# Two layers of a streaming encoder on one core: an earlier norm sum, seven PSUM banks for MLA's input projection, and a last down projection with tokens on partitions

## The chip, the cores and the metric

The kernel runs on one core of one Trainium2 chip. The metric is the device time of one execution in microseconds (us), the median over runs. TensorE is called PE in the rows of the profile (PEld is its weight load), VectorE DVE, ScalarE ACT, GpSimd POOL, and SyncE SP; SP issues all the DMAs spoken of here.

## The reference, cut to what matters

Two layers of an encoder trunk are computed for 256 prompt frames and for 8 sequences of 16 new frames with caches, together N = 384 tokens of D = 1024 features. All is float32.

```python
for layer in range(2):
    y = y + 0.5 * swiglu_ffn(y, ffn1_norm[layer], ffn1_w_gu[layer], ffn1_w_down[layer])
    h = rmsnorm(y, mix_norm[layer])
    if layer == 0: y = y + even_merge(a_attend(...), b_attend(...), ...)   # two kinds of attention
    else:                                                                # multi-head latent attention (MLA)
        cq, ckv, kr = split(h @ c_w_in, [384, 640])    # 384 | 256 | 32 columns
        q = rmsnorm(cq, g_q) @ w_q_up;  ckv = rmsnorm(ckv, g_kv);  kr = rope(kr)
        y = y + c_attend(q, expand(ckv), kr) @ c_w_out
    y = y + 0.5 * swiglu_ffn(y, ffn2_norm[layer], ffn2_w_gu[layer], ffn2_w_down[layer])
return rmsnorm(y, final_norm), and the new keys, values and latents

def swiglu_ffn(x, g, w_gu, w_down):                    # w_gu 1024 x 5632, w_down 2816 x 1024
    gate, up = split(rmsnorm(x, g) @ w_gu, 2)
    return (silu(gate) * up) @ w_down
```

## The kernel before, in words

Activations lie transposed: the residual is eight SBUF tiles x0 to x7, each 128 features by 384 tokens. Each float32 product is made as three matmuls in a faster format: both operands are split into a high and a low part (h and l in the names: xh, xl for normed-to-be activations, wh, wl for weights, gh, gl for the gated values), and `mm3` adds h·h, h·l and l·h into one PSUM bank. ACT makes the high part (CAST, or ACTIVATE with the norm's gain as scale), DVE the low part by subtraction. `load_w` does this for a weight block of 128 x 1024: a DMA into one of three raw buffers, then cast and subtraction into one of three split buffers.

A norm is applied late. `Sub.push` scales x by the gain alone and adds its square to `ssq` (class `Stats`). `Stats.rstd` then sums over the partitions by a float32 matmul of ones with ssq into the PSUM bank T and makes 1/sqrt on DVE and ACT (`ms`, a root on ACT, a reciprocal and four small steps on DVE). The projections go on meanwhile and are multiplied by rstd when DVE reads them from PSUM. So until rstd is there, every finished projection holds its bank.

PSUM has eight banks: three named acc, two S, two L, one T. `acc_tile` hands out the three acc banks in turn, and `ring_tile` hands out all seven.

The four FFNs are one function, `ffn`. It runs over the 22 blocks f of 128 hidden features: a gate and an up projection of 24 matmuls each (8 feature blocks by 3), then g = gate·rstd on DVE, Silu on ACT, u = up·rstd and u·silu on DVE, and the split into gh, gl. The first two projections run interleaved (`pair`). In the very first FFN four run interleaved (`together`), as the weights arrive, and the call of `rstd` stands behind the first further pair. The squares of this first norm are made on POOL (`push(d, True)`), all others on ACT with the sum on POOL. The down projection then runs over the 8 output blocks d of 128 features: 22 x 3 matmuls of 384 columns with the weights as the stationary operand, and DVE adds half of the result to x[d].

In `mla_mixer` five projections of c_in (three for cq, two for ckv) and a narrow one for kr precede a chain on DVE: rstd, cq, ckv, their norms' sums (`rc_m`), a reciprocal root by integer start and three Newton steps (`rc_t`, `rc_o`), and `spread`, which makes diagonal tiles `dg` that a float32 matmul with ones turns into rows (bank acc). The query-up projections (cqh, cql with q_up weights) are next on TensorE, and DVE can read them only when `te` and `to`, made from the spread, are there.

After the last FFN the final norm sums the squares over features with small matmuls, spreads 1/rms over the partitions, and DVE multiplies eight tiles y, each followed by its store (1.5 KB runs, transposed on the host afterwards).

The tile framework orders the instructions of each engine by its own simulation, within the bounds of data and buffers; engines then run their queues in order.

Of the kernel before, what the change touches and what calls it, by code (L numbers as in the profile page):

```python
# [11 lines left out]
F32 = mybir.dt.float32  # L12
F32R = mybir.dt.float32r
I32 = mybir.dt.int32
AF = mybir.ActivationFunctionType
# [20 lines left out]
LAM_INIT = 0.8 - 0.6 * math.exp(0.0)  # L36
CH = 1024

G_FFN1, G_MIX, G_FFN2, G_FIN, G_CQ, G_CKV, G_SUB = 0, 16, 32, 48, 56, 59, 61
G_N = 62  # L40
C_ID, C_COMB, C_BM, C_M0, C_TE, C_TO = 0, 128, 192, 200, 202, 586
C_N = 970

# [23 lines left out]
def trunk(ctx, tc, I, O):  # L67
# [13 lines left out]
    def acc_tile():  # L81
        return ps_a.tile([P, 512], F32, name="acc")
# [72 lines left out]
    def rsqrt(out, ms, shape):  # L155
        r, n = shape
        t = tmp.tile([P, N], F32, name="rs_t", bufs=1)[:r, :n]
        nc.scalar.sqrt(t, ms)
        nc.vector.reciprocal(out, t)  # L159
        nc.vector.tensor_tensor(out=t, in0=ms, in1=out, op=ALU.mult)  # L160
        nc.vector.tensor_tensor(out=t, in0=t, in1=out, op=ALU.mult)
        nc.vector.tensor_scalar(t, t, -0.5, 1.5, op0=ALU.mult, op1=ALU.add)
        nc.vector.tensor_tensor(out=out, in0=out, in1=t, op=ALU.mult)
# [64 lines left out]
    class Sub:  # L228
# [4 lines left out]
            self.g = g  # L233

        def push(self, d, onpool=False):
            if self.g is None:
                if d < KT - 1:
                    self.stats.add(x[d])
                return
            h = nrm.tile([P, N], F32R, name=f"xh{d}", tag=f"xh{d}")  # L240
            l = nrm.tile([P, N], F32R, name=f"xl{d}", tag=f"xl{d}")
            g = gcol(self.g + d)
            nc.scalar.activation(h, x[d], AF.Copy, scale=g)
            nc.vector.scalar_tensor_tensor(l, x[d], g, h.bitcast(F32), op0=ALU.mult, op1=ALU.subtract)  # L244
            self.h[d], self.l[d] = h, l
            self.stats.add(x[d], onpool)
# [18 lines left out]
    def pair(sub, w0, w1, new=ring_tile):  # L265
        return together(sub, lambda k: (blk(w0, k), blk(w1, k)), new)
# [2 lines left out]
        nc.vector.scalar_tensor_tensor(x[d], ps[:, :N], coef, x[d], op0=ALU.mult, op1=ALU.add)  # L269


    def ffn(sub, gu, down, g_next, pre=()):
        with tc.tile_pool(name="ffn", bufs=1) as fp, tc.tile_pool(name="ffnt", bufs=2) as ft:
            gt = []
            held = []
            rstd = None
            if pre:
                g0, u0, g1, u1 = together(sub, lambda k: [blk(pre[k // 2], 4 * (k % 2) + c) for c in range(4)])
                held = [(0, g0, u0), (1, g1, u1)]
            for f in range(len(held), FT):  # L280
                wg = load_w(gu[2 * f])
                if f == 0:
                    held.append((0, *pair(sub, wg, load_w(gu[1]))))
                    continue
                pg = proj(sub, wg, new=ring_tile)
                pu = proj(sub, load_w(gu[2 * f + 1]), new=ring_tile)
                held.append((f, pg, pu))
                if rstd is None:
                    rstd = sub.stats.rstd(D)
                for f_, pg, pu in held:  # L290
                    g = ft.tile([P, N], F32, name="g")
                    s = ft.tile([P, N], F32, name="s")
                    u = ft.tile([P, N], F32, name="u")
                    nc.vector.tensor_tensor(out=g, in0=pg[:, :N], in1=rstd, op=ALU.mult)  # L294
                    nc.scalar.activation(s, g, AF.Silu)
                    nc.vector.tensor_tensor(out=u, in0=pu[:, :N], in1=rstd, op=ALU.mult)
                    nc.vector.tensor_tensor(out=u, in0=u, in1=s, op=ALU.mult)
                    h = fp.tile([P, N], F32R, name=f"gh{f_}")
                    l = fp.tile([P, N], F32R, name=f"gl{f_}")
                    split(u, h, l)  # L300
                    gt.append((h, l))
                held = []
            nxt = Sub(g_next)
            for d in range(KT):
                ps = ring_tile()
                for c0 in range(0, FT, 8):
                    n = min(8, FT - c0)
                    w = load_w(down[d][:, c0 * P:(c0 + n) * P], n * P)
                    for j in range(n):
                        k = c0 + j  # L310
                        mm3(ps[:, :N], blk(w, j), gt[k], k == 0, k == FT - 1)
                add_resid(ps, d, 0.5)
                nxt.push(d)
            return nxt
# [298 lines left out]
    def mla_mixer(sub, g_next):  # L613
        with ExitStack() as es:
# [15 lines left out]
            cst = Stats()  # L630
            cqs = []
            slot = lambda shape, dt, name, tag: mp.tile(shape, dt, name=name, tag=tag)
            two = pair(sub, load_w(I["c_in"][0]), load_w(I["c_in"][1]), acc_tile)
            for i in range(3):
                ps = two.pop(0) if two else proj(sub, load_w(I["c_in"][i]))
                if rstd is None:
                    rstd = sub.stats.rstd(D)
                t = slot([P, N], F32, f"cq{i}", ("oh7", "ol7")[i % 2])
                nc.vector.tensor_tensor(out=t, in0=ps[:, :N], in1=rstd, op=ALU.mult)  # L639
                cst.add(t)  # L640
                g = gcol(G_CQ + i)
                h = slot([P, N], F32R, f"cqh{i}", f"oh{i}")
                l = slot([P, N], F32R, f"cql{i}", f"ol{i}")
                nc.scalar.activation(h, t, AF.Copy, scale=g)
                nc.vector.scalar_tensor_tensor(l, t, g, h.bitcast(F32), op0=ALU.mult, op1=ALU.subtract)
                cqs.append((h, l))
# [2 lines left out]
            cks = [(slot([P, NP], F32R, f"ckvh{i}", f"oh{3 + i}"), slot([P, NP], F32R, f"ckvl{i}", f"ol{3 + i}"))  # L649
                   for i in range(2)]  # L650
            for i in range(2):
                ps = proj(sub, load_w(I["c_in"][3 + i]))
                nc.vector.tensor_tensor(out=ckv[:, i], in0=ps[:, :N], in1=rstd, op=ALU.mult)
                kst.add(ckv[:, i])
            w = load_w(I["c_kr"], 512)
# [191 lines left out]

    sub = Sub(G_FFN1)
    for d in range(KT):
        sub.push(d, True)  # L850
    nc.sync.dma_start(out=con, in_=I["con"])
    sub = ffn(sub, I["gu0"], I["dn0"], G_MIX, first_w)
    sub = even_mixer(sub, G_FFN2)
    sub = ffn(sub, I["gu1"], I["dn1"], G_FFN1 + 8)
    sub = ffn(sub, I["gu2"], I["dn2"], G_MIX + 8)
    sub = mla_mixer(sub, G_FFN2 + 8)
    sub = ffn(sub, I["gu3"], I["dn3"], None)
    sq = tmp.tile([P, N], F32, name="sq")
    nc.scalar.sqrt(sq[:, 0:1], ones[:, 0:1])
    nc.scalar.activation(sq, x[KT - 1], AF.Square)  # L860
    pc = acc_tile()
    sub.stats.sums(pc, 0, stop=False)
    sub.stats.sums(pc, 0, sq, start=False)
    ms = tmp.tile([P, 16], F32, name="rc_m")[:, :3]
    nc.vector.tensor_scalar(ms, pc[:, :3], 1.0 / D, EPS, op0=ALU.mult, op1=ALU.add)
    rc = nrm.tile([P, 16], F32, name="rc_o", bufs=2)[:, :3]
    rsqrt(rc, ms, (P, 3))
    rb = spread(rc, 0)
    for d in range(KT):
        y = nrm.tile([P, N], F32, name=f"y{d}", tag=f"xh{d}")  # L870
        nc.vector.scalar_tensor_tensor(y, x[d], gcol(G_FIN + d), rb[:, :N], op0=ALU.mult, op1=ALU.mult)  # L871
        nc.sync.dma_start(out=O["y"][d * P:(d + 1) * P], in_=y)

# [24 lines left out]
def _host(i):  # L900
# [2 lines left out]
    o = {}  # L903
    xx = np.concatenate([A["x_prompt"][0], A["x_sample"].reshape(NS, D)], 0)
    o["xT"] = f(xx.T.reshape(KT, P, N).transpose(1, 0, 2))
    cols = [A["ffn1_norm"], A["mix_norm"], A["ffn2_norm"], A["final_norm"], A["c_q_norm"], A["c_kv_norm"], A["b_subln"]]
    o["gains"] = f(np.concatenate([a.reshape(-1, P) for a in cols], 0).T)
    o["con"] = _consts()
    for l in range(2):
        for n, nm in enumerate(("ffn1", "ffn2")):  # L910
            g = A[nm + "_w_gu"][l].reshape(KT, P, 2, FT, P).transpose(3, 2, 1, 0, 4)
            o[f"gu{2 * l + n}"] = f(g).reshape(2 * FT, P, KT * P)
            d = A[nm + "_w_down"][l].reshape(FT, P, KT, P).transpose(2, 1, 0, 3)
            o[f"dn{2 * l + n}"] = f(d).reshape(KT, P, FF)
    e = A["e_w_in"][0].reshape(KT, P, 6, 4, P)
    o["e_in"] = f(e[:, :, [0, 1, 3, 4]].transpose(2, 3, 1, 0, 4)).reshape(16, P, KT * P)
    o["e_v"] = f(e[:, :, [2, 5]].transpose(2, 1, 0, 3, 4)).reshape(2, P, KT * 512)
# [37 lines left out]
    return o  # L955


_OUT = {"y": (D, N), "ak": (512, N), "av": (N, 512), "bk": (512, N), "bv": (N, 512), "ckv": (256, N), "ckr": (32, N)}


# [21 lines left out]
```

## Time and profile before

| | |
|---|---|
| median of 3 runs | 1512.06 us (1512.0 to 1515.81) |
| the profiled execution | 1511.95 us, span 1510.2 us |
| busy: PE / DVE / ACT / POOL | 1481.2 / 793.7 / 591.1 / 135.9 us |
| mean granted clock of TensorE | 0.989 |

The span is from the first to the last instruction; the 1.75 us between it and the execution's time lie around the program. Busy time of TensorE is modelled and overlaps from one matmul to the next, so the distance between two starts tells more than a duration. The granted clock is the share of 2.4 GHz that TensorE was given; 0.5 is 1.2 GHz.

### The profile page before, as it was taken

Reading aid. Unit: us, or ns where it says so; the run is one execution under the profiler, and the core shown is the slowest. Engines: PE = TensorE matmul, PEld = TensorE weight load, DVE = VectorE, ACT = ScalarE, POOL = GpSimd, SP = SyncE. Lnnn points to the kernel's source line nnn. Section 1 sums busy time; section 2 is a strip of 40 time slices with the busy share of each in tenths; the row PEclk is TensorE's granted clock in tenths of the full one; section 3 lists DMA queues with packets and bytes.
Section 4 is the critical chain, followed back from the end, with each engine's and each line's share of the span. In section 5 each row is a group of like instructions: output and inputs, shape, how many; then the busy total and the mean of one; then the engine's idle time right before and its main releaser. Section 6 shows DMA issues by size and latency. Waiting matters only on the chain.

```text
span 1510.2 us, 21698 instructions
## 1 busy us (share of the span) xinstructions
PE 1481.2 (98%) x8680; PEld 1443.6 (96%) x8680; DVE 793.7 (53%) x1369; ACT 591.1 (39%) x996; POOL 135.9 (9%) x146
## 2 busy tenths in 40 slices
PE   9899999999999999999999999999899999999997
PEld 9899999998888999999999999999798999999997
DVE  6655543345356755553346555434757466555433
ACT  4433333325345433333334333333367444333231
POOL 5000000114230100000100000011210020000000
PEclk9999999999899999999999999999999999999998
DMA  7333343545443343344433334445231133433341
GB/s 239 110 125 126 126 126 115 171 149 175 145 133 105 120 132 126 126 124 124 129 126 126 126 126 127 124 120 180 86 125 38 62 119 127 130 129 124 116 130 66
DMA packets 71877, 190.09 MB, mean 126 GB/s; under 512 B 6720, under 2 KB 26848, under 8 KB 71392
## 3 DMA queue, kind: packets, MB, share of 16 engines
q1 hardware_dynamic: 71776, 188.71, 39.7%
q8 instruction: 68, 1.11, 0.3%
q14 instruction: 33, 0.27, 0.1%
HBM read 183.52 MB, written 5.16 MB: 125 GB/s over the span
## 4 chain that ended last, share of the span: by engine, by line
PE 95%; DVE 3%; issue 1%; ACT 1%; POOL 0%; DMA 0%; SPq 0%; DVEq 0%; ACTq 0%; POOLq 0%
PE acc L93 46%; PE L L93 24%; PE S L93 24%; PE T L352 1%; DVE wl L102 0%; PE T L93 0%; ACT wh L101 0%; POOL wl L102 0%; DMA raw<-gu 0%; DVE y L871 0%; DVE dg L182 0%; DVE xl L244 0%; DVE rstd L159 0%; DVE rc_t L173 0%; DVE bd L527 0%
## 5 line engine op out<-in xcount | busy, mean ns | idle before, releaser
L101 ACT CAST wh<-raw 128x1024 fp32r<-128x1024 f32 (+2 forms) x329 | 335.4, 1021 | 768.7 <-issue 290.6
L102 DVE TENSOR_TENSOR wl<-raw,wh 128x1024 fp32r<-128x1024 f32 (+2 forms) x313 | 375.5, 1201 | 271.0 <-ACT wh L101 267.1
L93 PE MATMUL acc<-xh,wh 128*128 128x384 f32 x752 | 253.6, 337 | 4.3 <-DVE cq L639 4.3
L93 PE MATMUL acc<-xh,wl 128*128 128x384 f32 x752 | 252.2, 335 | 0.0
L93 PE MATMUL acc<-xl,wh 128*128 128x384 f32 x752 | 252.2, 335 | 0.0
L202 POOL TENSOR_TENSOR ssq<-ssq,sq 128x384 f32<-128x384 f32 x44 | 51.9, 1179 | 1161.5 <-ACT sq L201 1161.3
L93 PEld LDWEIGHTS acc<-xh,wh 128*128 128x128 f32 x752 | 141.3, 188 | 6.4 <-issue 5.5
L93 PE MATMUL L<-xh,wh 128*128 128x384 f32 x424 | 142.6, 336 | 0.0
L93 PE MATMUL S<-xh,wh 128*128 128x384 f32 x408 | 137.2, 336 | 5.2 <-DVE g L294 4.4
L93 PEld LDWEIGHTS acc<-xl,wh 128*128 128x128 f32 x752 | 141.2, 188 | 1.0 <-issue 0.5
L93 PE MATMUL L<-xl,wh 128*128 128x384 f32 x424 | 141.6, 334 | 0.0
L93 PE MATMUL L<-xh,wl 128*128 128x384 f32 x424 | 141.6, 334 | 0.0
L93 PEld LDWEIGHTS acc<-xh,wl 128*128 128x128 f32 x752 | 141.2, 188 | 0.3
L93 PE MATMUL S<-xh,wl 128*128 128x384 f32 x408 | 137.1, 336 | 0.3 <-DVE wl L102 0.3
L93 PE MATMUL S<-xl,wh 128*128 128x384 f32 x408 | 137.0, 336 | 0.3 <-DVE xl L244 0.3
L93 PE MATMUL acc<-gh,wl 128*128 128x384 f32 x308 | 104.0, 338 | 0.0
L93 PE MATMUL acc<-gl,wh 128*128 128x384 f32 x308 | 104.0, 338 | 0.0
L93 PE MATMUL acc<-gh,wh 128*128 128x384 f32 x308 | 104.0, 338 | 0.0
L93 PEld LDWEIGHTS S<-xh,wh 128*128 128x128 f32 x408 | 77.1, 189 | 5.7 <-issue 4.7
L93 PEld LDWEIGHTS L<-xl,wh 128*128 128x128 f32 x424 | 79.6, 188 | 0.4
L93 PEld LDWEIGHTS L<-xh,wh 128*128 128x128 f32 x424 | 79.6, 188 | 0.4
L93 PEld LDWEIGHTS L<-xh,wl 128*128 128x128 f32 x424 | 79.6, 188 | 0.0
(299 smaller groups left out, 2488.5 us busy)
## 6 DMA issues: line engine op xcount, KB each, us to landing
raw<-gu SPq DMA_DIRECT2D x172, 512.0 KB, 3.3
raw<-dn SPq DMA_DIRECT2D x64, 512.0 KB, 3.5
raw<-dn SPq DMA_DIRECT2D x32, 384.0 KB, 3.1
raw<-e_in SPq DMA_DIRECT2D x16, 512.0 KB, 3.4
raw<-e_v SPq DMA_DIRECT2D x8, 512.0 KB, 3.9
raw<-e_out SPq DMA_DIRECT2D x8, 512.0 KB, 3.4
raw<-c_out SPq DMA_DIRECT2D x8, 512.0 KB, 3.7
raw<-q_up SPq DMA_DIRECT2D x8, 384.0 KB, 3.1
```

What stands on the lines that cost most here:

```text
L93: nc.tensor.matmul(out, lhsT=l, rhs=r, start=start, stop=stop)
L101: nc.scalar.copy(out=h, in_=src)
L102: (eng or nc.vector).tensor_tensor(out=l, in0=src, in1=h.bitcast(F32), op=ALU.subtract)
L202: nc.gpsimd.tensor_tensor(out=self.acc, in0=self.acc, in1=sq, op=ALU.add)
L352: nc.tensor.transpose(pt[:, j * P:(j + 1) * P], w[:, j * P:(j + 1) * P], ident)
```

## The change

1. The squares of the first norm go from POOL to ACT (the sum stays on POOL). In the first FFN `rstd` is called behind the four interleaved projections; in the others behind the first gate projection, before its up projection.
2. The five projections of MLA's c_in take `ring_tile` banks instead of `acc_tile` banks.
3. In the last FFN the factor 0.5 goes into u, and the down projection is made with tokens on partitions: gh, gl are the stationary operand in blocks of 128 tokens, the weights move in 512 columns, and six banks (3 token blocks by 2 halves) accumulate at once while k runs over the 22 hidden blocks. The residual enters the same banks by 24 PE transposes of x at k = 0. The last two k are run bank by bank. A square on ACT with a sum along the free dimension, a small chain on DVE and a scaling then make the final norm for each token block, and y is stored with tokens as rows (2 KB runs, two stores per block).

```diff
     def push(self, d, onpool=False):
-            if self.g is None:
-                if d < KT - 1:
-                    self.stats.add(x[d])
-                return
...
+    def down_tokens(fp, gt, down):
+        TT, HF = N // P, D // 512
+        gfin = fp.tile([P, D], F32, name="gfin")
+        GF = I["gfin"]
+        nc.sync.dma_start(out=gfin, in_=bass.AP(GF.tensor, GF.offset, [[0, P], [1, D]]))
+        ps = [[ring_tile() for _ in range(HF)] for _ in range(TT)]
+
+        def residual(t):
+            for d in range(KT):
+                j = d % 4
+                nc.tensor.matmul(ps[t][d // 4][:, j * P:(j + 1) * P], lhsT=x[d][:, t * P:(t + 1) * P], rhs=ident,
+                                 start=j == 0, stop=False, is_transpose=True)
+
+        def add(t, k, w, halves=range(HF)):
+            hs = [a[:, t * P:(t + 1) * P] for a in gt[k]]
+            for hf in halves:
+                wb = blk(w, hf, 512)
+                mm(ps[t][hf], hs[0], wb[0], False, False)
+                mm(ps[t][hf], hs[0], wb[1], False, False)
+                mm(ps[t][hf], hs[1], wb[0], False, k == FT - 1)
+
+        eps = fp.tile([P, 1], F32, name="eps")
+        nc.vector.memset(eps, EPS)
+        nc.scalar.sqrt(fp.tile([P, 1], F32, name="dummy"), eps)
+        sm = fp.tile([P, TT, HF], F32, name="fs")
+        ys = [fp.tile([P, D], F32, name=f"y{t}") for t in range(TT)]
+
+        def half(t, hf):
+            sq = fp.tile([P, 512], F32, name="fq", bufs=2)
+            nc.scalar.activation(sq, ps[t][hf], AF.Square, accum_out=sm[:, t, hf:hf + 1])
+            sl = slice(hf * 512, hf * 512 + 512)
+            nc.vector.tensor_tensor(out=ys[t][:, sl], in0=ps[t][hf], in1=gfin[:, sl], op=ALU.mult)
+
+        def finish(t):
+            c = fp.tile([P, 4], F32, name=f"fc{t}")
+            ms, rt, nh, rc = [c[:, i:i + 1] for i in range(4)]
+            nc.vector.tensor_scalar(ms, sm[:, t, 0:1], sm[:, t, 1:2], 1.0 / D, op0=ALU.add, op1=ALU.mult)
+            nc.scalar.activation(rt, ms, AF.Sqrt, bias=eps)
+            nc.vector.tensor_scalar(nh, ms, EPS, -0.5, op0=ALU.add, op1=ALU.mult)
+            nc.vector.reciprocal(rc, rt)
+            nc.vector.scalar_tensor_tensor(rt, rc, nh, rc, op0=ALU.mult, op1=ALU.mult)
+            nc.vector.scalar_tensor_tensor(rc, rt, 1.5, rc, op0=ALU.add, op1=ALU.mult)
+            y = ys[t]
+            nc.scalar.activation(y[:, :512], y[:, :512], AF.Copy, scale=rc)
+            nc.sync.dma_start(out=O["y"][t * P:(t + 1) * P, :512], in_=y[:, :512])
+            nc.vector.tensor_scalar(y[:, 512:], y[:, 512:], rc, None, op0=ALU.mult)
+            nc.sync.dma_start(out=O["y"][t * P:(t + 1) * P, 512:], in_=y[:, 512:])
+
+        late = 2
+        for k in range(FT - late):
+            w = load_w(down[k])
+            for t in range(TT):
+                if k == 0:
+                    residual(t)
+                add(t, k, w)
+        ws = [load_w(down[k]) for k in range(FT - late, FT)]
+        for t in range(TT):
+            for hf in range(HF):
+                for k, w in zip(range(FT - late, FT), ws):
+                    add(t, k, w, [hf])
+                half(t, hf)
+            finish(t)
...
                 held = [(0, g0, u0), (1, g1, u1)]
+                rstd = sub.stats.rstd(D)
...
                 pg = proj(sub, wg, new=ring_tile)
+                if rstd is None:
+                    rstd = sub.stats.rstd(D)
                 pu = proj(sub, load_w(gu[2 * f + 1]), new=ring_tile)
                 held.append((f, pg, pu))
-                if rstd is None:
-                    rstd = sub.stats.rstd(D)
...
+                    if g_next is None:
+                        nc.vector.scalar_tensor_tensor(u, pu[:, :N], 0.5, rstd, op0=ALU.mult, op1=ALU.mult)
...
+            if g_next is None:
+                down_tokens(fp, gt, down)
+                return None
...
-            two = pair(sub, load_w(I["c_in"][0]), load_w(I["c_in"][1]), acc_tile)
+            two = pair(sub, load_w(I["c_in"][0]), load_w(I["c_in"][1]))
...
-                ps = two.pop(0) if two else proj(sub, load_w(I["c_in"][i]))
+                ps = two.pop(0) if two else proj(sub, load_w(I["c_in"][i]), new=ring_tile)
...
-                ps = proj(sub, load_w(I["c_in"][3 + i]))
+                ps = proj(sub, load_w(I["c_in"][3 + i]), new=ring_tile)
...
-        sub.push(d, True)
+        sub.push(d)
...
-    sub = ffn(sub, I["gu3"], I["dn3"], None)
-    sq = tmp.tile([P, N], F32, name="sq")
...
+    ffn(sub, I["gu3"], I["dn3"], None)
```

On TensorE, in the first FFN, behind the four interleaved projections (xh_199 and xl_200 are the last feature block, T<-ssq,ones is the norm's sum, S is the first bank of the next projection):

```order
 L93 MATMUL acc<-xl_200,wh 128x384
 L93 MATMUL acc<-xh_199,wl 128x384
+L93 MATMUL T<-ssq,ones 128x384
 L93 MATMUL S<-xh_152,wh 128x384
 L93 MATMUL S<-xl_153,wh 128x384
...
 L93 MATMUL L<-xl_200,wh 128x384
 L93 MATMUL L<-xh_199,wl 128x384
-L93 MATMUL T<-ssq,ones 128x384
 L93 MATMUL acc<-xh_152,wh 128x384
```

The sum moved from behind the next gate and up projection to before them, past 48 matmuls.

On TensorE in MLA, where the spread's matmuls (dg) stand among the query-up projections (cqh, cql; nine matmuls make one). Between the six small sums and dg stood 33 of these matmuls before; now 28 do:

```order
 L93 MATMUL L<-cql_9484,wh 128x384
 L93 MATMUL L<-cqh_9483,wl 128x384
-L93 MATMUL acc<-dg,ones 128x128 x6
+L93 MATMUL L<-cqh_9523,wh 128x384
+L93 MATMUL L<-cql_9524,wh 128x384
+L93 MATMUL L<-cqh_9523,wl 128x384
+L93 MATMUL S<-cqh_9474,wh 128x384
+L93 MATMUL acc<-dg,ones 128x128 x5
+L93 MATMUL acc<-cqh_9474,wh 128x384
```

The spread comes five matmuls earlier in the stream, and one of its six matmuls stands behind five more of a projection. (On DVE, the subtraction of the fourth q_up block, which stood inside the Newton steps, now stands behind the fifth dg.)

On ACT at the end of the program before, behind the last cast (x_126 and x_129 are the last two residual tiles):

```order
L201 ACTIVATE sq<-x_126 128x384
L859 ACT_TABLE_LOAD
L859 ACTIVATE sq<-ones 128x1
L860 ACTIVATE sq<-x_129 128x384
L158 ACTIVATE rs_t<-rc_m 128x3
```

And on ACT at the end of the changed program, behind the last cast (fq, fs are a square and its sum, fc the small columns of a token block, y_12867 to y_12869 the three token blocks):

```order
L297 ACTIVATE fq,fs<-acc 128x512
L297 ACTIVATE fq,fs<-L 128x512
L297 ACTIVATE fq,fs<-acc 128x512
L305 ACT_TABLE_LOAD
L305 ACTIVATE fc_13404<-fc_13404,eps 128x1
L297 ACTIVATE fq,fs<-S 128x512
L297 ACTIVATE fq,fs<-L 128x512
L311 ACTIVATE y_12867<-y_12867,fc_13404 128x512
L297 ACTIVATE fq,fs<-acc 128x512
L305 ACTIVATE fc_13433<-fc_13433,eps 128x1
L305 ACTIVATE fc_13462<-fc_13462,eps 128x1
L311 ACTIVATE y_12868<-y_12868,fc_13433 128x512
```

Where two squares and two roots stood, there are six, three and three scalings. The scaling of the first block stands before the last square, and a table load stands before the first root, although the code asks for a root ahead of the stage: that one was placed at the FFN's start, before its Silus. 

## Rows read from the trace of the kernel before

**Rows 1.** The page, first part: busy time and share of the span, instructions.
```profile
PE 1481.2 (98%) x8680; PEld 1443.6 (96%) x8680; DVE 793.7 (53%) x1369; ACT 591.1 (39%) x996; POOL 135.9 (9%) x146
```

**Rows 2.** TensorE's waits: us in total, times, longest us.
```profile
PE acc L93 <- DVE dg L182: 4.9, 3, 2.4
PE S L93 <- DVE g L294: 4.4, 1, 4.4
PE acc L93 <- DVE cq L639: 4.3, 1, 4.3
```

**Rows 3.** Stretches, first FFN: length, PE busy (instructions), granted clock, DMA share, GB/s.
```profile
43.06:46.40 3.34, 3.34 (x11) 0.51 0.34 132
...
48.80:61.30 12.50, 12.50 (x74) 1.00 0.30 92
```

**Rows 4.** Timeline of DVE, first FFN: start, length, instruction, idle before and releaser.
```profile
34.49 0.56 DVE L209 TENSOR_SCALAR ms<-T 128x384 f32<-128x384 f32 x1 [2.67 <-PE T L93]
...
42.36 0.56 DVE L294 TENSOR_TENSOR g<-S,rstd 128x384 f32<-128x384 f32 x1
```

**Rows 5.** The start: POOL's last sum (timeline), and a stretch of ACT alone.
```profile
25.15 1.88 POOL L196 TENSOR_TENSOR ssq<-ssq,sq 128x384 f32<-128x384 f32 x1
...
6.00:16.60 10.60, 8.20 (x12) 1.00 1.09 341
```

**Rows 6.** Stretches in MLA: PE, PEld, DVE, ACT, POOL busy, granted clock, DMA share, GB/s.
```profile
1063.20:1067.10 3.90, 3.89 (x13) 3.90 (x14) 3.23 (x6) 2.88 (x6) 2.00 (x2) 0.56 0.02 6
...
1084.50:1087.00 2.50, 0.17 (x1) 0.00 (x0) 2.29 (x10) 0.00 (x0) 0.00 (x0) 1.00 0.00 0
1087.00:1091.10 4.10, 4.08 (x18) 4.08 (x19) 3.58 (x10) 0.41 (x1) 0.16 (x1) 0.58 0.32 100
```

**Rows 7.** Timeline of DVE in MLA.
```profile
1062.51 1.02 DVE L639 TENSOR_TENSOR cq<-acc,rstd 128x384 f32<-128x384 f32 x2
...
1077.56 0.55 DVE L661 TENSOR_TENSOR kr<-acc,ktab 32x384 f32<-32x384 f32 x1 [2.46 <-PE acc L93]
...
1078.79 0.16 DVE L225 TENSOR_SCALAR rc_m<-acc 128x3 f32<-128x3 f32 x1
...
1085.21 0.96 DVE L102 TENSOR_TENSOR wl<-raw,wh 128x768 fp32r<-128x768 f32 x1
```

**Rows 8.** The last down projection as a stretch; PE's timeline in a value projection.
```profile
1404.10:1497.00 92.90, 92.90 (x529) 92.90 (x529) 30.23 (x32) 26.99 (x32) 7.26 (x6) 1.00 0.35 103
...
338.18 0.39 PE L93 MATMUL acc<-wh,xh 128*128 128x512 f32 x1
...
341.58 0.39 PE L93 MATMUL acc<-wh,xh 128*128 128x512 f32 x1
```

**Rows 9.** PE's timeline with transposes (L352), and the stretch around it.
```profile
444.03 0.49 PE L352 MATMUL T<-con,e 128*128 128x128 f32 x3
444.35 0.86 PE L93 MATMUL L<-pT,vb 128*128 128x32 f32 x7
...
442.00:450.00 8.00, 8.00 (x75) 6.53 (x73) 6.03 (x20) 3.74 (x11) 2.74 (x3) 1.00 0.59 177
```

**Rows 10.** The end: timeline of DVE and ACT; the stores' issues and landings.
```profile
1497.24 0.56 DVE L269 SCALAR_TENSOR_TENSOR x<-acc,x 128x384 f32<-128x384 f32 x1 [9.96 <-PE acc L93]
...
1486.82 1.28 ACT L859 ACT_TABLE_LOAD   x1
...
L872 SPq DMA_DIRECT2D o_y<-y x8: 332/332/344, 1503.4 to 1507.1; - x8
...
DMA to landing us min/median/max: 1.9/1.9/2.0
```

**Rows 11.** Groups of ACT and DVE by form: busy us, mean ns of one, idle before.
```profile
L458 ACT ACTIVATE v_a<-acc,rc_o 128x512 f32<-128x512 f32 x3 | 2.0, 689 | 1.6 <-PE acc L93 1.6
...
L325 ACT ACTIVATION_READ_ACCUMULATOR e<-sS,nm 128x1 f32 x64 | 12.2, 191 | 0.0
...
L162 DVE TENSOR_SCALAR rs_t<-rs_t 128x384 f32<-128x384 f32 x5 | 1.8, 358 | 0.1
```

More of the change, by code (lines that the diff above doesn't have):

```diff
@@ L37 @@
 CH = 1024
-G_FFN1, G_MIX, G_FFN2, G_FIN, G_CQ, G_CKV, G_SUB = 0, 16, 32, 48, 56, 59, 61
-G_N = 62
+G_FFN1, G_MIX, G_FFN2, G_CQ, G_CKV, G_SUB = 0, 16, 32, 48, 51, 53
+G_N = 54
 C_ID, C_COMB, C_BM, C_M0, C_TE, C_TO = 0, 128, 192, 200, 202, 586
@@ L295, in ffn @@
                     nc.scalar.activation(s, g, AF.Silu)
-                    nc.vector.tensor_tensor(out=u, in0=pu[:, :N], in1=rstd, op=ALU.mult)
+                    if g_next is None:
+                        nc.vector.scalar_tensor_tensor(u, pu[:, :N], 0.5, rstd, op0=ALU.mult, op1=ALU.mult)
+                    else:
+                        nc.vector.tensor_tensor(out=u, in0=pu[:, :N], in1=rstd, op=ALU.mult)
                     nc.vector.tensor_tensor(out=u, in0=u, in1=s, op=ALU.mult)
@@ L856, in trunk @@
     sub = mla_mixer(sub, G_FFN2 + 8)
-    sub = ffn(sub, I["gu3"], I["dn3"], None)
-    sq = tmp.tile([P, N], F32, name="sq")
[L859 to L872, printed above, removed]
+    ffn(sub, I["gu3"], I["dn3"], None)
 T5_EDGES = np.array([1, 2, 3, 4, 5, 6, 7, 8, 12, 16, 23, 32, 46, 64, 91])
@@ L905, in _host @@
     o["xT"] = f(xx.T.reshape(KT, P, N).transpose(1, 0, 2))
-    cols = [A["ffn1_norm"], A["mix_norm"], A["ffn2_norm"], A["final_norm"], A["c_q_norm"], A["c_kv_norm"], A["b_subln"]]
+    cols = [A["ffn1_norm"], A["mix_norm"], A["ffn2_norm"], A["c_q_norm"], A["c_kv_norm"], A["b_subln"]]
     o["gains"] = f(np.concatenate([a.reshape(-1, P) for a in cols], 0).T)
@@ L914, in _host @@
             o[f"dn{2 * l + n}"] = f(d).reshape(KT, P, FF)
+    o["dn3"] = f(A["ffn2_w_down"][1]).reshape(FT, P, D)
+    o["gfin"] = f(A["final_norm"]).reshape(1, D)
     e = A["e_w_in"][0].reshape(KT, P, 6, 4, P)
@@ L955, in _host @@
     return o
-_OUT = {"y": (D, N), "ak": (512, N), "av": (N, 512), "bk": (512, N), "bv": (N, 512), "ckv": (256, N), "ckr": (32, N)}
+_OUT = {"y": (N, D), "ak": (512, N), "av": (N, 512), "bk": (512, N), "bv": (N, 512), "ckv": (256, N), "ckr": (32, N)}
 def kernel(**inputs):
@@ L972 @@
     g = {k: np.asarray(r["o_" + k]) for k in _OUT}
-    T = {k: np.ascontiguousarray(g[k].T) for k in ("y", "ak", "bk", "ckv", "ckr")}
-    T["av"], T["bv"] = g["av"], g["bv"]
+    T = {k: np.ascontiguousarray(g[k].T) for k in ("ak", "bk", "ckv", "ckr")}
+    T["y"], T["av"], T["bv"] = g["y"], g["av"], g["bv"]
     shp = {"ak": (8, 64), "av": (8, 64), "bk": (4, 128), "bv": (4, 128), "ckv": (256,), "ckr": (32,)}
```

## The prediction

> **What bounds the kernel now.** I read the page's first part, then who waits for whom on TensorE, then busy time and granted clock in the stretches around the longest waits, then the last 15 us engine by engine. TensorE is busy for 1481.2 of 1510.2 us [rows 1]. So a saving is worth its size only if it shortens TensorE's own stream, closes a hole in it, or shortens what follows its last matmul. The profiled execution took 1511.95 us with a span of 1510.2, and the median of the three runs is 1512.06, so the sum below is made from 1511.95.
>
> The holes are few. The three longest entries among TensorE's waits are one wait of 4.4 us for DVE's g (first FFN), one of 4.3 us for cq (MLA), and three waits for dg (spreads), the longest 2.4 us [rows 2]. The first two cost more than their length. The matmuls behind the first, from 43.06 to 46.40, have a granted clock of 0.51, the lower level of 1.2 GHz; from 48.80 on the clock is 1.00 (2.4 GHz), and 72 matmuls take 12.5 us, 0.1736 us each [rows 3]. So 3.34 us at half speed lose 3.34 x (1 - 0.51) = 1.6 us, and the hole costs 4.4 + 1.6 = 6.0. In MLA 3.9 us at 0.56 follow the hole [rows 6] and lose 1.7: 4.3 + 1.7 = 6.0. The third loss is the end: DVE picks up the last down matmul at 1497.24 [rows 10] and the span ends at 1510.2, 12.9 us later.
>
> **First FFN: the norm sum.** The order shows the ssq matmul (T) behind four projections instead of six, so 48 matmuls or 48 x 0.1736 = 8.3 us earlier. DVE's chain from it runs from ms at 34.49 to the end of the first g at 42.92, 8.4 us [rows 4]. Moved up, ms starts near 26.2 and that g ends near 34.6. The projection that reuses g's bank wants it at 43.06 - 4.4 = 38.6: 4.0 us in hand. The next banks fall free one DVE instruction apart (0.56 us, as for g), while TensorE asks for one each 24 x 0.1736 = 4.2 us. The hole and its slow stretch go: **-6.0**. Bounds: -3.0 (ACT's casts and table load come to lie before the root and eat the 4.0 us and 1.4 more, and the clock falls all the same) to -6.2.
>
> The sum must be there for it. Before, POOL made squares and sums and ended at 25.15 + 1.88 = 27.0 [rows 5], behind the new place of T (near 25.4). Now ACT makes eight squares and POOL seven adds. A square of 384 columns is some 0.52 us, by its columns from the 0.69 of a 512-column ACTIVATE [rows 11], so eight are 4.2 us. ACT had 10.6 - 8.2 = 2.4 us free between 6 and 16.6 [rows 5]; the last cast of x then ends some 2 us later, near 18.5, where TensorE wants it with the last 12 of the 96 matmuls, from about 23. POOL's last add follows a us or two later, 4 us before T. This is the cover, and without it up to 2 us of ACT's work would be on the path. DVE gets back what POOL no longer takes part in: **-0.2**, bounds -0.6 (the short waits at the start) to +2.
>
> In the other FFNs the same edit moves T one projection forward. No wait of TensorE stands there: 0.
>
> **MLA: seven banks.** The five projections of c_in take ring banks, so the fourth no longer waits for cq0, read from its bank at 1062.51 [rows 7]. TensorE goes on through the fourth, the fifth and the key projection, each in a bank that nobody holds. **-6.0**, if the next wait doesn't grow. What is late next is dg. From rc_m at 1078.79 [rows 7] to TensorE's restart at 1087.0 [rows 6] are 8.2 us, which 33 matmuls fill up to 1084.5. In the new order 28 stand before dg: 5 x 0.1755 = 0.9 us less cover. But the 0.96 us weight subtraction inside DVE's chain [rows 7] now stands behind five of the six dg: 0.96 less chain. The two cancel: 0. If the chain kept its length, +0.9; if the idle gets so short that the clock stays up (4.1 us at 0.58 lose 1.7 now [rows 6]), -1.7. Bounds for MLA -4.0 to -7.7.
>
> **The last down projection.** Before: 8 x 22 x 3 = 528 matmuls of 384 columns in 92.9 us, 0.176 each [rows 8]. After: 22 x 3 x 2 x 3 = 396 of 512 columns, the same 202,752 columns. Such matmuls, with activations as the stationary operand, stand in the value projection: fifteen from 338.18 to 341.58, 0.2267 each [rows 8]. 396 x 0.2267 = 89.8. If the 2.4 ns by which down's matmuls exceed those of gate and up (0.176 against 0.1736) come with gh, 396 x 0.229 = 90.7. To this come 24 transposes of 128x128 for the residual: three take from 444.03 to 444.35, 0.11 each, or at most 0.16 by their 0.49 as a group [rows 9]. So 2.6 us, at most 3.9; I take 0.11, since they stand eight in a row. 90.2 (the middle) + 2.6 - 92.9 = **-0.1**; bounds -0.5 to +1.7. Loads are covered as before: 512 KB per 18 matmuls (4.1 us), where it was 512 KB per 24 (4.2 us). The load of gfin is one more row in SP's queue, in the sixth place of this FFN, with three buffers ahead of it: 0. The eight residual adds, seven squares and six POOL adds that go lay beside matmuls: 0.
>
> Here a rule speaks against the change. The row: from 442 to 450, a stretch with transposes among short matmuls, the granted clock is 1.00 [rows 9]. The Trainium skill (TensorE: Matmul & The Clock Gate, Part 4: PE-mode transpose) says that a transpose does not count as activity for the clock. By that, three groups of eight could let it fall; by the row they do not, and the sum has 0 for it. What a fall would cost is rival 2.
>
> **The end.** Let 0 be the moment when the last matmul can be read; the six banks finish 6 x 0.2267 = 1.36 us apart. By the order, ACT runs three squares, a table load (1.28 [rows 10]), a root, two squares, the first scaling, and then the last square. One square of 512 columns is taken as 0.69 and its accumulator read as 0.19 [rows 11], so ACT comes 0.7 late and the last sum is there at 1.5. DVE's last product ends at 1.8; then, at 0.2 each, block 1's reciprocal and block 2's mean (2.2, and ACT's root at 2.4), three small ones for block 1 and half a row of it (0.36 for 384 columns [rows 11], so 0.43) to 3.2, three for block 2 to 3.8. ACT's last scaling (at most 0.69) ends at 4.5. SP issues two stores, the second near 4.9. A store lands 2.0 us after its issue, and the span ended 1.1 us after the last landing (1507.1 + 2.0) [rows 10]; 0.2 more for 256 instead of 192 KB: 8.2. 8.2 - 12.9 = **-4.7**. Bounds: -6.8 (nothing queues behind block 1: 6.1) to -3.0 (all of block 1's work lies before block 2's).
>
> **Sum.** -6.0 - 0.2 - 6.0 - 0.1 - 4.7 = -17.0, and 1511.95 - 17.0 = 1495.0. With every term at its good end it is 1490.2, with every one at its bad end 1505.7.
>
> **Rivals.** (1) A hole only moves. In MLA all that follows hangs on DVE; were it busy when rc_m is due, TensorE would wait at dg for most of what it saved. For it: TensorE already waits there. Against: DVE idles 2.46 us before kr even now [rows 7], and the same work is due. Price 6: 1501. The same if the first FFN's hole comes back a bank later. (2) The clock falls behind the transposes. Each group of eight then costs what the slow stretch in rows 3 loses, 1.6: +4.8, 1499.8. Against it: rows 9. (3) The edits don't do what they say: T waits for its sum, the stores queue, the new end is as long as the old one. Then 1508 to 1512. Against: both holes have a named cause, and the order shows it gone. (4) Slower: the clock stays low through the new down stage, whose runs over six banks are short. At 1.2 GHz a 512-column matmul takes 512/2.4 ns = 0.21 us more: 80 of the 396 eat the gain, 102 make it slower by over 0.3%, all give 1579. For it no row speaks, only the rule above. Against: the value projection runs in this form over three banks at full speed [rows 8].
>
> **Chances.** Forecast 0.65 (its own range 1490 to 1498.5), rival 1 0.16, rival 2 0.08, rival 3 0.07, rival 4 0.04. A difference up to 0.3% (4.5 us) cannot be told from none. The forecast and rivals 1 and 2 are faster, 0.89; rival 3 the same, 0.07; rival 4 slower, 0.04. The range for 8 in 10 covers the forecast and rivals 1 and 2: 1489.5 to 1502.
>
> **What would show it.** Right: no wait for g near 38 or for cq near 1059, and the clock at 1.00 in both places; 396 matmuls in about 90 us behind 3 us of transposes at 1.00; 8 us from the last matmul to the end, with one table load among the squares. Wrong: a new wait for T or for an operand before 25, an idle stretch over 4 us before dg, a down stage over 96 us, an end over 10 us.

## The result, and the profile after

The changed kernel takes 1496.37 us (median of 4, 1493.38 to 1498.98) against 1513.93 (1512.0 to 1516.22): ratio 0.9883, interval 0.9857 to 0.9909. The profiled execution has a span of 1494.6 and a clock of 0.993. The page's first part and TensorE's longest waits:

```profile
PE 1476.4 (99%) x8554; PEld 1422.4 (95%) x8554; DVE 786.4 (53%) x1367; ACT 595.1 (40%) x1011; POOL 119.6 (8%) x132
```

```profile
PE acc L93 <- DVE dg L182: 3.2, 2, 2.5
PE L L93 <- DVE bd L594: 2.5, 1, 2.5
PE S L93 <- DVE xl L240: 1.0, 1, 1.0
```

The waits for g and cq of [rows 2] are gone; dg kept its wait, 2.5 where it was 2.4. The first FFN by timeline (POOL's last sums, DVE's chain), then as stretches (PE, PEld, DVE, ACT, POOL busy, clock, DMA share, GB/s):

```profile
14.42 6.44 POOL L202 TENSOR_TENSOR ssq<-ssq,sq 128x384 f32<-128x384 f32 x4 [0.53 <-ACT sq L201]
26.36 0.56 DVE L209 TENSOR_SCALAR ms<-T 128x384 f32<-128x384 f32 x1 [2.29 <-PE T L93]
34.23 0.56 DVE L355 TENSOR_TENSOR g<-S,rstd 128x384 f32<-128x384 f32 x1
```

```profile
26.00:34.00 8.00, 8.00 (x47) 7.87 (x47) 7.13 (x8) 4.73 (x5) 0.00 (x0) 1.00 0.56 199
34.00:48.00 14.00, 14.00 (x82) 14.00 (x81) 11.90 (x21) 7.76 (x13) 0.00 (x0) 1.00 0.47 151
...
1071.20:1074.00 2.80, 0.39 (x3) 0.07 (x1) 2.53 (x10) 0.83 (x1) 1.05 (x1) 1.00 0.00 0
1074.00:1078.20 4.20, 4.16 (x18) 4.03 (x19) 2.89 (x8) 0.00 (x0) 0.00 (x0) 0.59 0.25 80
...
1392.12:1486.77 94.65, 94.65 (x421) 77.03 (x419) 29.84 (x33) 26.76 (x34) 0.00 (x0) 1.00 0.30 98
```

The sum is there 4.7 us ahead of T; where [rows 3] had a hole and a clock of 0.51, TensorE is busy throughout at 1.00. In MLA the idle stretch before dg and the slow one behind it stand as in [rows 6]. The new down stage is 94.65 long, where [rows 8] has 92.90. PE's timeline shows eight transposes, 1394.39 to 1395.18:

```profile
1394.39 0.60 PE L278 MATMUL acc<-con,x 128*128 128x128 f32 x4
1394.82 0.60 PE L278 MATMUL S<-con,x 128*128 128x128 f32 x4
1395.18 0.48 PE L93 MATMUL acc<-wh,gh 128*128 128x512 f32 x1
```

The end, by the timelines of ACT, DVE and SP's queue:

```profile
1483.56 1.28 ACT L305 ACT_TABLE_LOAD   x1
1485.06 0.58 ACT L297 ACTIVATE fq<-S 128x512 f32<-128x512 f32 x1
1485.65 0.60 ACT L297 ACTIVATE fq<-L 128x512 f32<-128x512 f32 x1
1486.23 0.71 ACT L311 ACTIVATE y<-y,fc 128x512 f32<-128x512 f32 x1
1487.03 0.60 ACT L297 ACTIVATE fq<-acc 128x512 f32<-128x512 f32 x1
1487.75 0.69 DVE L299 TENSOR_TENSOR y<-acc,gfin 128x512 f32<-128x512 f32 x1
1488.42 0.20 DVE L304 TENSOR_SCALAR fc<-fs 128x1 f32<-128x1 f32 x1
1490.03 0.72 ACT L311 ACTIVATE y<-y,fc 128x512 f32<-128x512 f32 x1 [0.32 <-DVE fc L309]
1489.88 1.23 SPq L312 DMA_DIRECT2D o_y<-y  x2
1491.21 0.40 SPq L314 DMA_DIRECT2D o_y<-y  x1
```

### The profile page after: what moved, and what is told of

Its sections match the earlier page's. It is cut to its first block, busy times and chain, and to the rows that moved or that the text cites. A ratio compares the mean times of both kernels' runs of the same rounds, so it can differ in the third digit from the quotient of the medians.

```text
span 1494.6 us, 21409 instructions
## 1 busy us (share of the span) xinstructions
PE 1476.4 (99%) x8554; PEld 1422.4 (95%) x8554; DVE 786.4 (53%) x1367; ACT 595.1 (40%) x1011; POOL 119.6 (8%) x132
## 4 chain that ended last, share of the span: by engine, by line
PE 95%; DVE 1%; issue 1%; ACT 1%; POOL 0%; DMA 0%; SPq 0%; ACTq 0%; DVEq 0%; POOLq 0%
PE acc L93 45%; PE L L93 25%; PE S L93 24%; PE T L419 1%; PE T L93 0%; DMA raw<-gu 0%; POOL wl L102 0%; DVE dg L182 0%; ACT wh L101 0%; ACT fq L297 0%; DVE rc_t L173 0%; DVE bd L594 0%; DVE wl L102 0%; DVE rc_t L169 0%; PE T L847 0%
## 5 line engine op out<-in xcount | busy, mean ns | idle before, releaser
L93 PE MATMUL acc<-xh,wh 128*128 128x384 f32 x728 | 245.3, 337 | 0.0
L93 PE MATMUL acc<-xl,wh 128*128 128x384 f32 x728 | 243.8, 335 | 0.0
L93 PE MATMUL acc<-xh,wl 128*128 128x384 f32 x728 | 243.8, 335 | 0.0
L93 PE MATMUL S<-xh,wh 128*128 128x384 f32 x432 | 145.2, 336 | 0.5 <-ACT xh L239 0.5
L93 PE MATMUL S<-xl,wh 128*128 128x384 f32 x432 | 144.7, 335 | 1.0 <-DVE xl L240 1.0
L93 PE MATMUL S<-xh,wl 128*128 128x384 f32 x432 | 144.5, 334 | 0.0
L93 PEld LDWEIGHTS acc<-xh,wh 128*128 128x128 f32 x728 | 136.3, 187 | 1.8 <-issue 0.9
L93 PEld LDWEIGHTS S<-xl,wh 128*128 128x128 f32 x432 | 81.1, 188 | 1.7 <-DVE xl L240 1.3
L93 PEld LDWEIGHTS S<-xh,wl 128*128 128x128 f32 x432 | 81.1, 188 | 0.0
L93 PE MATMUL acc<-gl,wh 128*128 128x384 f32 x220 | 74.4, 338 | 0.0
```

The source lines that it names most:

```text
L93: nc.tensor.matmul(out, lhsT=l, rhs=r, start=start, stop=stop)
```

## The experiments

Executions of one and the same order differ by up to some 3 us at the start and in the first mixer, so each run is read by stretches of its own trace. The table gives them, worked out from starts in PE's timelines: the first matmul on S to the first mixer's dg; the last matmul on MLA's T to the first on ckvh; the start of the first instruction of the last down stage to that of its last; from there to the end.

| | first FFN | MLA | last down | end | span |
|---|---|---|---|---|---|
| before | 298.44 | 55.38 | 92.76 | 13.31 | 1510.2 |
| changed | 292.20 | 49.40 | 94.42 | 8.03 | 1494.6 |
| u1_late_sum | 299.61 | 49.49 | 94.43 | 8.03 | 1503.0 |
| u2_three_banks | 291.88 | 55.44 | 94.43 | 8.03 | 1501.4 |
| u3_old_down | 291.92 | 49.32 | 92.75 | 13.30 | 1497.4 |
| e_keys_on_act | 292.08 | 45.31 | 94.43 | 8.02 | 1490.8 |
| e_tail | 291.91 | 49.44 | 94.42 | 7.51 | 1496.4 |
| e_best | 292.60 | 45.32 | 94.39 | 7.50 | 1489.0 |

**The parts, each undone alone.**

```diff
 u1:  rstd() behind the next gate and up projection again, push(d, True)
 u2:  -two = pair(..., load_w(I["c_in"][1]))
      +two = pair(..., load_w(I["c_in"][1]), acc_tile)   (and the others without new=ring_tile)
 u3:  the kernel before with the first two parts
```

> The changed kernel with its first part alone undone: the squares of the first norm on POOL again, the norm's sum behind the next gate and up projection again. If the part is worth what its wait and the slow stretch behind it cost (the trace of before: 4.4 idle and 1.6 lost at the lower clock), TensorE waits over 4 us for DVE's g near 38, the clock falls behind it, and the span is 1494.6 + 6.0 = 1500.6. If the gain came from something else, or the hole had only moved, the span stays within 1 us of 1494.6.

> The changed kernel with its second part alone undone: MLA's five input projections in the three acc banks again. If the fourth projection waits for cq's bank as before, a wait of 4.3 us and a slow stretch come back near 1053 and the span is 1494.6 + 6.0 = 1500.6; the wait for dg, 2.5 in the changed kernel, keeps its length within 0.5. Rival (what is saved at the bank is paid again at dg): the span moves by less than 2 us, because the wait for dg shrinks by as much.

> The kernel before with the first two parts of the change: the third is undone (down projection with the weights stationary, final norm over features). By the changed kernel's trace the new down stage is 1.75 us longer than the old one and the new end 5.4 us shorter, so the span is 1494.6 - 1.75 + 5.4 = 1498.2, with the down stage at 92.9 and 13 us from the last down matmul to the end. By the terms of the prediction (-0.1 and -4.7) it would be 1499.4. If the parts depend on one another, the two stretches differ from 92.9 and 13.2 by over 1 us.

Times: u1 1502.74, u2 1502.36, u3 1500.49, with 1512.41 for the kernel before; ratios 0.9931 (0.991 to 0.9952), 0.9929 (0.99 to 0.9957) and 0.992 (0.9893 to 0.9947). Waits and stretches of u1, then of u2, then the two stretches of u3:

```profile
PE S L93 <- DVE g L354: 4.4, 1, 4.4
```

```profile
44.30:49.00 4.70, 4.65 (x15) 4.68 (x16) 4.70 (x11) 2.53 (x6) 0.00 (x0) 0.50 0.26 98
```

```profile
PE acc L93 <- DVE cq L706: 4.3, 1, 4.3
PE acc L93 <- DVE dg L182: 3.1, 2, 2.3
```

```profile
1058.00:1062.00 4.00, 4.00 (x14) 4.00 (x15) 3.33 (x6) 2.81 (x6) 2.04 (x2) 0.57 0.02 4
```

```profile
1391.36:1484.30 92.94, 92.94 (x530) 92.94 (x530) 30.21 (x32) 26.97 (x32) 7.28 (x6) 1.00 0.35 103
1484.30:1497.41 13.11, 3.19 (x19) 2.72 (x18) 6.51 (x18) 0.73 (x2) 0.00 (x0) 0.60 0.34 120
```

Each part gives back its own stretch and leaves the others alone. u1 costs 7.4 in the first FFN, 1.4 more than the 6.0 expected; 0.7 of that is the clock, which this time stayed at 0.50 for 4.7 us behind the hole (2.3 lost, not 1.6), and the rest was not traced. u2 costs 6.0 with an unchanged wait for dg, so rival 1 is out. u3 costs 3.6 (-1.7 and +5.3), so the sum of the prediction's last two terms was 1.2 too good.

**The early sum with POOL's squares** (`sub.push(d, True)` alone).

> The changed kernel with the norm's sum early, as now, but the squares of the first norm on POOL again. In the kernel before, POOL's last sum ended at 27.0, and T is due at 25.5 now. If ACT's squares are what makes the early sum possible, TensorE waits for POOL's ssq for 1.6 us near 25.5, and the span grows by that, to 1496.2; the wait for g does not come back, because the bank is wanted 13 us behind T and the first g ends 9 us behind it. If POOL is faster without the other engines' pressure, there is no wait and no difference.

```profile
24.61 1.88 POOL L196 TENSOR_TENSOR ssq<-ssq,sq 128x384 f32<-128x384 f32 x1
27.41 0.81 PE L93 MATMUL T<-ssq,ones 128*128 128x384 f32 x2
```

No wait came, against what was expected. POOL's last sum ended at 26.49, 5.6 later than ACT's squares allow, but this execution's clock was low at the start (0.91 from 7.70 to 27.41), so T came due only at 27.41. With the changed kernel's start (T at 25.51) a wait of 1.0 would be due; the run shows that the early call makes the gain without ACT's squares, and leaves open what these add. The span was 1495.3, the time 1497.12 (one run).

**The transposes, four times over.**

```diff
-                if k == 0:
-                    residual(t)
+                for i in range(4 if k == 0 else 0):
+                    residual(t, i < 3)
```

> The changed kernel with the 24 transposes of the residual made four times over (each time anew, so that the result stays the same): 72 more of them, in groups of 32. At the 0.10 us that they took in the changed kernel (1394.39 to 1395.18 for eight) 72 cost 7.2 us and the span is 1501.8, if the granted clock stays at 1.00 through the groups. If transposes don't hold the clock up (rival 2 of the prediction), a group of 32 is 3 us long and the matmuls behind it run at the lower clock: 0.21 us more for each 512-column matmul there, so 1.3 us for each group of six matmuls and more behind the last, a span over 1504 and clocks under 1.00 between 1392 and 1410.

```profile
1400.00:1404.00 4.00, 4.00 (x36) 3.90 (x35) 0.00 (x0) 0.00 (x0) 0.00 (x0) 1.00 0.02 4
1404.00:1412.00 8.00, 8.00 (x36) 6.50 (x35) 2.45 (x2) 2.10 (x2) 0.00 (x0) 1.00 0.18 66
```

From 1399.93 to 1403.34 TensorE does nothing but 32 transposes, and the clock is 1.00 there and behind them. The stage grew by 7.86, 0.109 for each of the 72; the time was 1502.25 (one run), the span 1500.5. Rival 2 is out.

**Why 0.2325 and not 0.2267.** Three runs on the matmul of 512 columns.

> Two edits to the changed kernel. The last down projection takes the tiles xh, xl in place of gh, gl as stationary operand for k = 0 to 7 (the first eight blocks of the gated values are left out of the result, so this tells of time alone), and the pool of small tiles is opened ahead of the pool that holds xh and xl, which moves xh6, xl6, xh7 and xl7 from the bytes below 98,000 of an SBUF partition to those from 99,744 to 105,888; gh and gl stay at 107,552 and above. Theory 1: a 512-column matmul takes 0.2325 instead of 0.2267 because of where its activations lie in SBUF. Then k = 0 to 5 run at 0.227, k = 6 and 7 and all gh blocks at 0.2325, the down stage is 108 x 0.0055 = 0.6 us shorter, and in gate and up projections the matmuls on blocks 6 and 7 take 0.176 where the others take 0.1735 (that is +12 x 0.0025 us for each projection, 1.3 us for each FFN's 44, some 6 us on the span). Theory 2: it is how gh and gl are made, or which pool they are from: k = 0 to 7 all at 0.227, gate and up unchanged. Theory 3: it is the stage itself (three matmuls to a bank, then the next of six): all k at 0.2325.

> The changed kernel, with the tiles gh, gl of the last FFN left where they are and filled differently: for blocks 0 to 7 with the scaled x (made as xh, xl are made, an ACTIVATE with a scale and a DVE scalar_tensor_tensor), for blocks 8 to 15 with x itself (made as gh, gl are, a CAST and a subtraction), from 16 on as before. (Sixteen of the 22 gated blocks are so left out of the result; the run tells of time alone.) A 512-column matmul takes 0.2325 on gh, gl and 0.2267 on xh, xl. If it is the place in SBUF, at 107,552 and above, all 22 blocks stay at 0.2325 and the stage at 94.65. If it is how the tile is made, blocks 0 to 7 take 0.2267 and the others 0.2325: stage 0.8 us shorter. If it is the values that stand in the tile, blocks 0 to 15 take 0.2267: 1.7 us shorter.

> The changed kernel with the same instructions in the same order on every engine, and other addresses: the pools of constants, of the residual, of the raw weights and of small tiles are laid at the top of SBUF, so that gh0 to gl11 lie below byte 107,264 of a partition (70,400 to 105,728), and gh12 to gl21 from there to 136,448; xh, xl and the split weights stay low. In the changed kernel all gh, gl lie at 107,552 and above; their matmuls start 0.176 apart (384 columns) and 0.2325 (512 columns), those on xh, xl 0.1736 and 0.2267. Theory: the place of the activations sets it, with a border between 105,888 and 107,552. Then k = 0 to 11 of every down projection run at 0.1736 and 0.2267 and the others as before: three times 288 x 0.0024 = 2.1 us in the first three FFNs, 216 x 0.0058 = 1.25 in the last, something in the mixers, 3.4 to 4 us in all, span near 1491. Rival: it is the pool or the order of the stage; then nothing moves (span 1494 to 1497).

```diff
 e_operand:  -down_tokens(fp, gt, down)
             +down_tokens(fp, [sub.k(i) for i in range(KT)] + gt[KT:], down)      (and tmp opened ahead of nrm)
 e_contents: +if g_next is None and f_ < KT: ACTIVATE and scalar_tensor_tensor of x[f_] into h, l
             +elif g_next is None and f_ < 2 * KT: split(x[f_ - KT], h, l)
 e_layout:   -cons = pool("cons")
             +cons = pool("cons", side="right")      (resid, wraw and tmp too)
```

PE's timeline of e_operand where xh ends and gh begins, then one block of e_contents (x in the tiles gh, gl) and one of e_layout (gh low):

```profile
1426.81 0.39 PE L93 MATMUL L<-wh,xl 128*128 128x512 f32 x1
...
1427.49 0.40 PE L93 MATMUL acc<-wh,xl 128*128 128x512 f32 x1
1427.72 0.40 PE L93 MATMUL acc<-wh,gh 128*128 128x512 f32 x1
...
1428.42 0.39 PE L93 MATMUL L<-wh,gh 128*128 128x512 f32 x1
```

```profile
1401.78 0.40 PE L93 MATMUL acc<-wh,gl 128*128 128x512 f32 x1
...
1403.16 0.40 PE L93 MATMUL L<-wh,gl 128*128 128x512 f32 x1
```

```profile
1404.76 0.40 PE L93 MATMUL acc<-wh,gh 128*128 128x512 f32 x1
...
1406.15 0.40 PE L93 MATMUL L<-wh,gh 128*128 128x512 f32 x1
```

In e_operand the step is sharp: 0.2267 on xh, xl (k = 0 to 7, xh6 and xh7 in their higher place too), 0.2325 from the first matmul on gh (1427.72), and the stage is 93.66 by the table's measure, 0.76 shorter. So it is not the stage. In e_contents six starts take 1.38, 0.23 each, with x in the tiles, and the stage keeps its 94.42: neither the values nor the way they are made. In e_layout (same order of instructions, 1498.26 us, span 1499.0; the first FFN is 3.2 longer, with a clock of 0.94 up to 28) six take 1.39 on low tiles, and the stage takes 94.39: not the low or high place.

Of the theories only the pool is left, and with it the byte at which its tiles start. By the addresses that the program lays out, every fast pair of 384 or 512 columns has its activation tile and its weight tile starting at the same byte modulo 256 (xh and weights: 160 and 160; in e_layout 128 and 128), and every slow pair starts 128 apart (gh: 32 and 160; in e_layout 0 and 128). No run moved that start alone, so the cause is open.

**The keys' copies on ACT.** DVE and POOL of the changed kernel before dg:

```profile
1068.20 1.85 DVE L169 TENSOR_SCALAR rc_t<-rc_m 128x6 int32<-128x6 int32 x1
1070.52 1.75 DVE L173 SCALAR_TENSOR_TENSOR rc_t<-rc_t,rc_m 128x6 f32<-128x6 f32 x1
1072.70 0.17 DVE L173 SCALAR_TENSOR_TENSOR rc_t<-rc_t,rc_m 128x6 f32<-128x6 f32 x1
...
1067.94 2.08 POOL L770 COPY ko<-kr 64x2048 f32<-64x2048 f32 x1 [2.43 <-ACT kr L733]
1070.32 1.93 POOL L769 COPY ke<-kr 64x2048 f32<-64x2048 f32 x1
```

```diff
-            nc.gpsimd.tensor_copy(out=ke[64:128], ...)      (and ko[0:64])
+            nc.scalar.copy(out=ke[64:128], ...)
```

> The changed kernel with MLA's two copies that spread the rotated key over the heads (64 x 2048, into ke and ko) on ACT instead of POOL. In the changed kernel two small DVE instructions of the reciprocal root take 1.85 and 1.75 us at 1068.20 and 1070.52, where the same ones take 0.17 a little later, and POOL's two copies stand at 1067.94 and 1070.32 for 2.08 and 1.93. Theory: DVE's instructions wait for POOL's copies. Then both take 0.2, dg is ready some 3.2 us earlier, the wait of TensorE for dg (2.5) goes and the clock stays at 1.00 behind it (1.7): the span is 1494.6 - 4.2 = 1490.4 (down to -2.5 if the clock falls all the same). Rival: these two are long for a reason of their own (an integer operation and the first multiply in a new format); then they stay long, and the span is within 1 us of 1494.6. A loss is possible too: ACT's casts of the next weights come up to 4 us later, and TensorE could wait for those.

The same two in that run, and MLA's stretch (1048.20 to 1097.60 in the changed kernel, with TensorE busy for 46.95 of 49.40 and a clock of 0.97):

```profile
1068.66 0.15 DVE L169 TENSOR_SCALAR rc_t<-rc_m 128x6 int32<-128x6 int32 x1
1069.25 0.17 DVE L173 SCALAR_TENSOR_TENSOR rc_t<-rc_t,rc_m 128x6 f32<-128x6 f32 x1
```

```profile
1048.66:1093.97 45.31, 45.31 (x268) 44.08 (x266) 38.92 (x71) 22.22 (x30) 9.82 (x21) 1.00 0.44 139
```

As the theory had it: both are short, TensorE is busy through the whole stretch at 1.00, and MLA is 4.1 shorter (4.2 expected). The time was 1492.58 us, beside 1512.33 for the kernel before, one run each.

**The end.**

```diff
+        nc.scalar.activation(dummy, ws[-1][0][:, :1], AF.Sqrt, bias=eps, scale=0.0)   (instead of the sqrt ahead)
+        (nc.scalar if t == TT - 1 else nc.sync).dma_start(... y[:, :512])
```

> The changed kernel with two edits at its end: the root that loads ACT's table stands behind the last weights' cast instead of at the FFN's start, and the last block's first store goes through ACT's queue instead of SP's. In the changed kernel a table load of 1.28 stands between the third square and the first root at 1483.56, and SP issues the last three stores from 1489.88 to 1491.6. If the load sets the end, block 1 is done by the time the last bank is, DVE makes the last mean without waiting for block 1's steps, and the end (from the last matmul's start at 1486.54 to 1494.57, 8.0) gets 1.5 us shorter: span 1493.1. If only the stores' queue counts, 0.4. If the last chain (square, mean, root, four small steps, scaling, store, landing) is bound by itself, nothing.

```profile
1490.42 0.68 DVE L298 TENSOR_TENSOR y<-acc,gfin 128x512 f32<-128x512 f32 x1
...
1492.23 0.72 ACT L310 ACTIVATE y<-y,fc 128x512 f32<-128x512 f32 x1 [0.68 <-DVE fc L308]
1492.99 0.37 ACTq L311 DMA_DIRECT2D o_y<-y  x1
```

0.5 of the 1.5 came. Without the load block 1 is ready sooner, and its steps now stand ahead of the last product on DVE, which starts 1.48 behind the last matmul's start where it was 1.21. The last scaling starts 3.29 behind that start (3.49 in the changed kernel), which is 0.2 of the 0.5; the rest is put down to SP's queue, which no run changed alone. (The run's time, 1498.26, has a later first mixer in it: MLA's T stands at 1050.58, 2.4 behind the changed kernel's.)

**All that paid, together.**

> Three experiments put together: the copies of MLA's keys on ACT (-4.1 in its trace), the late table load and ACT's queue for one store (-0.5), and the other addresses (-3.4 to -4, if the place of the activations counts; nothing, if not). 1494.6 - 8 = 1486.5 of span if all three add, 1490 if the addresses do nothing. Against the kernel before: 24 us, a ratio of 0.984.

> The changed kernel once more, on the chip of the version that should beat it, for a fair distance between the two: 1496.4, and 8 us over that version.

1493.07 us (1489.25 to 1495.67), ratio 0.9866 (0.9844 to 0.9888); the changed kernel on the same chip 1497.5 (1494.89 to 1499.45), ratio 0.9896 (0.9876 to 0.9915), with 1514.32 for the kernel before. The distance of the two is 4.4, not 8, and their intervals overlap; the stretches (MLA -4.1, end -0.5) are the firm part. The addresses added nothing (last down 94.39), as the second branch of the expectation had it.

## Why the prediction was right

The forecast was 1495.0 us; 1496.37 was measured. By stretches of the two profiled executions the 15.6 us of span are -6.24 (first FFN), +0.21 (a later first matmul), -5.98 (MLA), and for the last part 102.45 instead of 106.07, -3.62. The forecast sum was -17.0. It came this close in part by luck: the last down projection was worse than forecast by 1.8 and the end better by 0.6.

**First norm sum, -6.0: right**, -6.24. T at 25.51, ms at 26.36 and the first g's end at 34.79 are within 0.2 of the times forecast, POOL's last add at 20.86 is 0.5 earlier; the hole goes with its slow stretch; u1 brings both back. That squares on ACT are what the early sum needs was not shown. **The start, -0.2: not seen.** The 96 matmuls ahead of T take 18.08 where they took 18.11, and the first one starts 0.21 later, no more than executions of one order differ there.

**MLA, -6.0: right**, -5.98, with the wait for dg at 2.5 and 4.2 us at 0.59 behind it: less cover and a shorter chain cancelled, as argued. What the prediction does not say is that 3.3 of the 8.2 us chain that it took as given were two stalls beside POOL's copies, which stood in the trace of the kernel before too:

```profile
1080.40 1.85 DVE L169 TENSOR_SCALAR rc_t<-rc_m 128x6 int32<-128x6 int32 x1
1082.72 1.75 DVE L173 SCALAR_TENSOR_TENSOR rc_t<-rc_t,rc_m 128x6 f32<-128x6 f32 x1
```

**The last down projection, -0.1: wrong by 1.8**, at its bound of +1.7 (94.42 instead of 92.76 in the table). The transposes were sized rightly: eight take 0.79. The step that failed is the price of a matmul, "396 x 0.2267 = 89.8 ... 396 x 0.229 = 90.7". The 396 took 94.65 less 2.4 for the transposes and, in all, some 0.3 where the three groups meet a matmul: 92.0, 0.232 each. The surcharge of down's tiles was seen (2.4 ns at 384 columns) and carried over as if fixed; at 512 columns it is 5.8. The right price stood in the trace of the kernel before, in rows that the prediction does not use: MLA's matmuls of 512 columns on ckvh and ckvl, 21 from 1116.76 to 1121.64, start 0.232 apart.

```profile
1116.76 0.39 PE L93 MATMUL acc<-wl,ckvh 128*128 128x512 f32 x1
...
1121.64 0.39 PE L93 MATMUL acc<-wl,ckvh 128*128 128x512 f32 x1
```

**The end, -4.7: -5.3.** The step "ACT comes 0.7 late" failed: the first scaling was done at 1486.94, and ACT took up the last square at 1487.03, 0.1 behind the last matmul's end. The term that was too long is the square with its sum, 0.69 + 0.19: from the fourth square to the next and from that to the scaling (1485.06, 1485.65, 1486.23) it is 0.59 and 0.58. All that follows is 0.6 to 0.7 earlier than forecast.

**Rivals.** 1: u2 and u3 leave dg's wait at 2.3 to 2.5. 2 and 4: the clock is 1.00 through the whole down stage, and with four times the transposes. The Trainium skill (TensorE: Matmul & The Clock Gate, Part 4: PE-mode transpose) says that a transpose does not count as a busy TensorE in the same way. Here the traces disagree: 3.4 us of nothing but transposes ran at 1.00 with 1.00 behind them, where an idle stretch of 2.45 in MLA was followed by 0.59. 3: each part's stretch moved.

## What to carry to other kernels

Where a norm is applied late, put its sum as early in TensorE's order as its squares allow: a hole costs its length and then the slow stretch behind it, 1.6 to 2.3 us here. Before a chain of tiny DVE instructions is taken as given, look for one that takes ten times its twin's time, and for what POOL does just then. A price per matmul belongs to its tiles as well as to its shape: look through the whole trace for rows of the same shape on other tiles, and where there are none, bound it widely. The 2.4 ns scaled up by columns would have been 3.2, and 5.8 came.

## What the runs showed of the hardware

A DVE instruction on 128x6 took 1.85 and 1.75 us while a POOL copy ran, ending within 0.03 us of the copy's end, and 0.15 and 0.17 without it. This agrees with what the Trainium skill (SBUF — State Buffer, Who interferes with whom) says of the port pair that VectorE and GpSimd share: it is an exclusive lock, and in VectorE's 2-port modes whoever issues first has it for the whole instruction while the other is blocked. In which mode these two ran, no trace shows.

Float32 transposes of 128x128 back to back start 0.109 us apart, and 32 of them in a row held the clock at 1.00.

Matmuls of one form start 0.2267 or 0.2325 apart (384 columns: 0.1735 or 0.176) by the activation tile that they read, with the clock at 1.00 both times; why is open. An estimate: were all those on gh, gl of the fast kind, 1584 x 0.0025 + 396 x 0.0058 = 6.3 us would be saved.
